# Split weights loaded from the GpSimd queue, and the whole output projection's weights split ahead of time

## The chip, the cores and the metric

The kernel runs on one core of one Trainium2 chip. The metric is the device time of one execution in microseconds (us). Three timed executions of the kernel before took 1645.35, 1647.06 and 1647.79 us.

## What is computed

One layer of a hybrid decoder trunk, for a batch of one, 2048 tokens and a model width of 1024, all in float32. In short, without the two mixers' insides:

```python
h = rmsnorm(x, norm_pre)
proj = h @ w_in                                   # 1024 -> 6416 columns
...
y_ssd = rmsnorm(ssd(...) * silu(z_ssd), ssd_norm) # Mamba-2 chunked scan, 16 heads x 64, in 2 groups
y_sc = sc_b * causal_dwconv(sc_c * sc_h, sc_conv_w) * silu(z_sc)
mix = jnp.concatenate([y_ssd, y_sc], axis=-1) @ w_out      # 2048 -> 1024
x = x + rmsnorm(mix, norm_post)
gate = jax.nn.sigmoid(x @ w_ple_gate)             # 1024 -> 1024
return x + gate * (p_i @ w_ple_proj)              # 256 -> 1024
```

`rmsnorm` divides by the root of the mean square over the width and multiplies by a weight.

## The kernel before

Activations stand transposed: 128 of the width on the partitions, 512 tokens (`TG`) along a row; there are four token groups. A float32 product is made of three products of rounded halves: each operand is split into a high part (a cast to fp32r on ACT, L146, L215, L543) and a low part (a subtraction on DVE, L147, L216, L546), and TensorE (PE) runs high x high, high x low and low x high (`PASSES`). A product with a 512-token group is thus twelve matmuls for four 128x128 blocks of weights. A *piece* is the split pair of such four blocks, 512 KB.

The stages, in the order of time:

- The **start** (`first_input`): warm-up products on a constant tile (`warm`, 14 of them, L452), then the projection of the per-layer embeddings `p` (`A_ple`), while the first tokens come in and their squares are summed (L425).
- The **input projection**, in two blocks of 1024 tokens, as 2x2 Strassen-Winograd products (seven for eight): for each block thirteen groups of one or two output tiles, each with seven products. Its weights come raw from HBM over SP's queue and are split on the way. While the groups 1 to 9 of the second block run (without the one for the scan's B and C), the generator `later_weights` is advanced by seven steps a group: it combines and splits the gate's weights and stores the pieces in HBM (`sg_d`), then splits the half of the output projection's weights that belongs to the short convolution and stores these (`so_d`, two pieces for each output tile).
- The **scan**, with the first half of the output projection in between (`under`, products `os`, weights `ws_os` read from `so_d`); its results go to HBM (`part_d`).
- The **output projection's second half** (`out_proj`, products `mo`): for a pair of token groups, eight output tiles each, two at a time. Its weights (`ws_o`) are loaded raw and split for each of the two pairs. Each result is evacuated with the stored part by DVE (`x`, L1217), then squared (ACT) and added to `ssq` (DVE, L1223).
- The **post-norm** (`norm`, L1233): for each token group the column sums of `ssq`, as four products with one column of ones, then root and reciprocal; the result goes through HBM and is spread over the partitions. `residual` (L1247, L1250) then adds the input `xres`.
- The **gate** (`gate_seven`), again seven products for eight, for two pairs of token groups: 28 pieces each (`GATES`), all read from `sg_d`. `finish` adds (L1288), takes the tanh (L1286, L1289), multiplies with the projected embeddings `pe` and adds `x` (L1291, L1292), and stores the result.

What sets the order: `Weights` holds all weights of the kernel as one sequence (`seq`) and six slots. `next` hands out a piece and starts the loads for the slots that are free by then; a load waits until PE has read the slot's last piece. All these loads are on SP's queue, which issues in order: with the loads of `part`, `xres`, `pe` and of the raw activations (L864), and the stores of the output (L1293). From the output projection on, `plan` lists at which unit (a step of `out_proj` or of the gate) the steps of norm, residual and gate operands are issued. A scheduler at build time puts each engine's instructions in an order by its own model of their durations; where the code says "in the order of the trace", an added edge keeps it from moving an instruction ahead.

## Time and profile before

| | us |
|---|---|
| median of three executions | 1647.06 (1645.35 to 1647.79) |
| the profiled execution | 1644.86 |
| its span on the core | 1643.2 |
| PE busy | 1628.1 |
| DVE busy | 1272.1 |
| ACT busy | 805.4 |
| POOL (GpSimd) busy | 49.6 |

All rows are of one profiled execution. Times are in us from the start of the span, unless marked ns. PE is the matmul engine and PEld its weight load, which runs beside it; DVE is VectorE, ACT ScalarE, POOL GpSimd, SP SyncE; SPq marks what an engine's queue issues or waits for. A row of a group has the line of the kernel, the engine, the operation, the names of what it writes and reads, the count, busy us and mean ns; a row of one tile has minimum, median and maximum ns, and the first and the last start. In a row of the timeline come start, length, engine, line, operation, and in brackets the idle time before it with what ended it. Matmuls overlap, and their ends are modelled: the time of a matmul is read from the distance of starts.

### The profile page before, as it was taken

The page shows a single profiled execution, that of the slowest core. Times are in us where ns is not written, and L with a number is a line of the kernel's source. Part 1 is how long each engine was busy: PE and PEld are TensorE (multiplying, and loading weights), DVE is VectorE, ACT ScalarE, POOL GpSimd, SP SyncE. Part 2 cuts the span into 40 slices and gives each one's busy share as a digit, 9 for nine tenths or more (in the row PEclk, how much of TensorE's full clock was granted, in tenths as well). Part 3 has the DMA queues.
Part 4 walks back from the last instruction along what each step waited for, and adds up shares of the span by engine and source line. Part 5 has one row for each costly group of instructions (what it writes and reads, how often), then busy time and mean ns, then how long its engine had stood idle before and what let it go on. Part 6 is the DMA issues. An engine that isn't in the chain of part 4 may idle for free.

```text
span 1643.2 us, 22720 instructions
## 1 busy us (share of the span) xinstructions
PE 1628.1 (99%) x8264; PEld 1339.9 (82%) x8264; DVE 1272.1 (77%) x1909; ACT 805.4 (49%) x1450; POOL 49.6 (3%) x71
## 2 busy tenths in 40 slices
PE   9999999999999999999999999999999999999998
PEld 8888888888888888888888888888788788887786
DVE  6997777987769978878978668477787736687785
ACT  8663444434337444554545335557757424234342
POOL 0000000000000100010010001000000000000000
PEclk9999999999999999999999999999999999999999
DMA  9452321774225334645765226878888535547996
GB/s 316 152 198 79 102 99 59 257 240 163 79 71 184 111 127 169 219 143 167 243 214 195 66 66 224 306 268 311 294 304 319 200 102 183 162 155 258 317 319 219
DMA packets 135620, 314.72 MB, mean 192 GB/s; under 512 B 18762, under 2 KB 20298, under 8 KB 135508
## 3 DMA queue, kind: packets, MB, share of 16 engines
q1 hardware_dynamic: 128596, 296.49, 53.5%
q10 hardware_dynamic: 6912, 16.78, 2.6%
q8 instruction: 65, 1.06, 0.3%
q14 instruction: 47, 0.39, 0.1%
HBM read 221.81 MB, written 91.41 MB: 191 GB/s over the span
## 4 chain that ended last, share of the span: by engine, by line
PE 90%; DVE 4%; DMA 3%; ACT 1%; issue 1%; SPq 0%; ACTq 0%; DVEq 0%
PE mo L226 9%; PE os L825 8%; PE mg_X L1315 5%; PE mg_Y L1315 4%; PE py L825 2%; PE A_ple L226 2%; PE A_xs1X L322 1%; PE A_xs2X L322 1%; PE A_gc6X L322 1%; PE A_gb7X L322 1%; PE A_gb5X L322 1%; PE A_gc7X L322 1%; PE A_z3X L322 1%; PE A_xs3X L322 1%; PE A_gb6X L322 1%; PE A_gc5X L322 1%
## 5 line engine op out<-in xcount | busy, mean ns | idle before, releaser
L825 PE MATMUL os<-act_m,ws_os 128*128 128x512 f32 x768 | 183.2, 394 | 0.7 <-ACT A_z L757 0.7
L226 PE MATMUL mo<-act_m,ws_o 128*128 128x512 f32 x768 | 178.0, 392 | 2.2 <-DVE x L1217 2.2
L226 PEld LDWEIGHTS mo<-act_m,ws_o 128*128 128x128 f32 x768 | 142.9, 188 | 36.2 <-DVE x L1217 5.1
L825 PEld LDWEIGHTS os<-act_m,ws_os 128*128 128x128 f32 x768 | 141.8, 188 | 34.3 <-issue 4.2
L1315 PE MATMUL mg_X<-act_x2s,ws_g 128*128 128x512 f32 x384 | 90.8, 393 | 0.7 <-ACT gth L1286 0.7
L146 ACT CAST ws_A_gc<-wr_A_gc 128x512 fp32r<-128x512 f32 x96 | 59.8, 623 | 56.9 <-PE A_gc5X L322 8.3
L1315 PEld LDWEIGHTS mg_X<-act_x2s,ws_g 128*128 128x128 f32 x384 | 70.9, 188 | 18.6 <-ACT gth L1286 1.7
L147 DVE TENSOR_TENSOR ws_A_gb<-wr_A_gb,ws_A_gb 128x512 fp32r<-128x512 f32 x96 | 66.0, 687 | 25.6 <-ACT ws_A_gb L146 25.4
L146 ACT CAST ws_A_gb<-wr_A_gb 128x512 fp32r<-128x512 f32 x96 | 59.6, 621 | 49.2 <-PE A_cb0Y L322 4.3
L676 DVE SCALAR_TENSOR_TENSOR xo<-ux,cols,xo 128x1024 f32<-128x1024 f32 x60 | 76.6, 1280 | 5.0 <-ACT xo L672 3.9
L1077 ACT ACTIVATE m<-m,adt 128x128 f32<-128x128 f32 x256 | 78.4, 390 | 0.9
L147 DVE TENSOR_TENSOR ws_A_gc<-wr_A_gc,ws_A_gc 128x512 fp32r<-128x512 f32 x96 | 66.0, 687 | 12.7 <-ACT ws_A_gc L146 11.8
L1315 PE MATMUL mg_Y<-act_x2s,ws_g 128*128 128x512 f32 x288 | 67.9, 392 | 1.4 <-DVE x L1250 1.4
L1315 PEld LDWEIGHTS mg_Y<-act_x2s,ws_g 128*128 128x128 f32 x288 | 53.5, 188 | 14.1 <-DVE x L1250 1.8
L1080 DVE SCALAR_TENSOR_TENSOR m<-m,gsb 128x1024 f32<-128x1024 f32 x32 | 38.2, 1222 | 25.4 <-ACT m L1077 25.4
L1217 DVE TENSOR_TENSOR x<-mo,part 128x512 f32<-128x512 f32 x32 | 22.1, 689 | 41.2 <-PE mo L226 41.0
L146 ACT CAST ws_A_xs<-wr_A_xs 128x512 fp32r<-128x512 f32 x48 | 29.9, 623 | 42.5 <-PE A_gc3X L322 8.4
L146 ACT CAST ws_A_z<-wr_A_z 128x512 fp32r<-128x512 f32 x48 | 29.9, 623 | 41.1 <-DVE wr_A_z L199 12.9
L1222 ACT ACTIVATE sq<-x 128x512 f32<-128x512 f32 x28 | 17.7, 633 | 63.4 <-DVE x L1217 63.3
L215 ACT CAST act_m<-mraw 128x512 fp32r<-128x512 f32 x64 | 37.4, 620 | 22.0 <-DVE mraw L880 10.1
L147 DVE TENSOR_TENSOR ws_A_z<-wr_A_z,ws_A_z 128x512 fp32r<-128x512 f32 x48 | 32.9, 686 | 18.4 <-ACT ws_A_z L146 18.4
L226 PE MATMUL A_ple<-act_p,ws_p 128*128 128x512 f32 x192 | 46.0, 397 | 0.0
(523 smaller groups left out, 3721.6 us busy)
## 6 DMA issues: line engine op xcount, KB each, us to landing
ws_g<-sg_d SPq DMA_DIRECT2D x56, 512.0 KB, 4.9
wr_A_gc<-in_w_t_dram SPq DMA_DIRECT2D x64, 256.0 KB, 2.7
wr_A_gb<-in_w_t_dram SPq DMA_DIRECT2D x64, 256.0 KB, 2.8
ws_os<-so_d SPq DMA_DIRECT2D x32, 512.0 KB, 5.8
m<-acs_d SPq DMA_DIRECT2D x32, 512.0 KB, 6.3
sg_d<-A_gs SPq DMA_DIRECT2D x28, 512.0 KB, 3.8
ple_d<-A_pe SPq DMA_DIRECT2D x32, 256.0 KB, 4.3
wr_A_xs<-in_w_t_dram SPq DMA_DIRECT2D x32, 256.0 KB, 3.6
```

Of the source, the lines that this page charges most:

```text
L146: S.copy(sp[:, 0, :kn, :], raw[:, :kn, :])
L147: V.tensor_tensor(sp[:, 1, :kn, :], raw[:, :kn, :], sp[:, 0, :kn, :].bitcast(F32), ALU.subtract)
L215: S.copy(a[:, 0, :], src)
L226: TE.matmul(out, sp[:, a, (k0 + k) % 4, :], act[k0 + k][:, b, :], start=k0 + k == 0 and q == 0, stop=k0 + k == n - 1 and q == 2)
L322: self.product = TE.matmul(out, sp[:, a, k % 4, :], t[:, b, ts_], start=p in OPENS and k == 0 and q == 0, stop=k == nk - 1 and q == 2, ski ...
L676: V.scalar_tensor_tensor(o, u[:, q:q + TB], col(w0 + q), o, ALU.mult, ALU.add)
L825: inst = f(*a, **k)
L1077: S.activation(m[:, c, :], m[:, c, :], AF.Exp, bias=nacs[b][:, h, c:c + 1])
L1080: V.scalar_tensor_tensor(mf, mf, 1.0, s["gsb"][gr], ALU.min, ALU.mult)
L1217: evac.append(V.tensor_tensor(x2[d], ps[:, i, :], pt[:, i, :], ALU.add))
L1222: S.activation(sq, x2[d], AF.Square)
L1315: TE.matmul(out, sp[:, a, k, :], ops_[t, p][k][:, b, :], start=p in OPENS and m_ == 0, stop=m_ == 11, skip_group_check=True)
```

## The change

It does five things.

- **Pieces of the output projection.** `so_d` has four pieces for each output tile. `later_weights` splits and stores all of them, first those of the short convolution, then those of the scan; it is advanced in groups 1 to 11 instead of 1 to 9. In the output projection's second half, pieces are loaded ready-made instead of raw, so the splits there go.
- **The queue of the pieces.** The loads of these pieces and of the gate's pieces are issued by GpSimd instead of SP.
- **The norm's sums.** `ssq` is split as well, into two tiles in which the columns that one product needs stand side by side; each product is two fp32r matmuls with two columns of ones.
- **The start.** The first four raw weights of the embeddings' projection are loaded from ACT's queue; nine warm-up products instead of 14.
- **The end.** The last output tile is finished in two halves.

```diff
-    so_d = [dram.tile([2, P, 2, TG], F32, name=f"so_d{d}") for d in range(KD)]
+    so_d = [dram.tile([4, P, 2, TG], F32, name=f"so_d{d}") for d in range(KD)]
...
+    ones_r = const.tile([P, 2], F32R, name="ones_r")
+    S.copy(ones_r, ones_d[:, 0:2])
...
-    def stored(src, name):
-
-        return name, lambda sp: nc.sync.dma_start(sp.bitcast(F32).rearrange("p a k c -> p a (k c)"), src)
+    def stored(src, name, by=nc.sync):
+
+        return name, lambda sp: by.dma_start(sp.bitcast(F32).rearrange("p a k c -> p a (k c)"), src)
...
-    seq = [direct(w_p[d], f"p_{d}", praw) for d in range(KD)]
+    seq = [direct(w_p[d], f"p_{d}", praw, S if d < 4 else nc.sync) for d in range(KD)]
...
     for t in range(0, NG, 2):
-        seq += [stored(so_d[d][q], f"os{t}_{d}_{q}") for d in range(KD) for q in range(2)]
+        seq += [stored(so_d[d][q], f"os{t}_{d}_{q}") for d in range(KD) for q in (2, 3)]
     for t in range(0, NG, 2):
-        seq += [direct(w_o[d, :, 4 * q:4 * q + 4, :], f"o{t}_{d}_{q}", praw) for d in range(KD) for q in (0, 1)]
+        seq += [stored(so_d[d][q], f"o{t}_{d}_{q}", G) for d in range(KD) for q in (0, 1)]
     for t in range(0, NG, 2):
-        seq += [stored(sg_d[n][p - 1], f"g{t}_{p}_{n}") for p, n in GATES]
+        seq += [stored(sg_d[n][p - 1], f"g{t}_{p}_{n}", G) for p, n in GATES]
...
-            for _ in range(14):
+            for _ in range(9):
                 TE.matmul(warm[:, 0:P], ones_d, ones_d, start=True, stop=True)
...
-            for n in range(2 * KD + 3):
-                if n < 2 * KD:
-                    d, q = divmod(n, 2)
+            parts = [(d, q) for h in (2, 0) for d in range(KD) for q in (h, h + 1)]
+            for n in range(len(parts) + 3):
+                if n < len(parts):
+                    d, q = parts[n]
...
                 if n >= 3:
-                    d, q = divmod(n - 3, 2)
+                    d, q = parts[n - 3]
                     keep(so_d[d][q], ahead[n - 3], f"A_os{d}_{q}")
...
-            elif b and 0 < n < 10 and ("cb", 0) not in prs:
+            elif b and 0 < n < 12 and ("cb", 0) not in prs:
                 mean = (next(gw, None) for _ in range(7))
...
                 ssq = ssq_[tg].rearrange("k (p c) -> k c p", c=TG // P)
+                hi, lo = (praw.tile([P, 4, P], F32R, tag="wraw", name=f"ssq2{n}_{tg}") for n in ("h", "l"))
+                S.copy(hi, ssq)
+                V.tensor_tensor(lo, ssq, hi.bitcast(F32), ALU.subtract)
                 ps = mm_bank(f"pn2_{tg}")
                 for c in range(TG // P):
-                    TE.matmul(ps[:, c:c + 1], ssq[:, c, :], ones_d[:, 0:1], start=True, stop=True)
+                    for n, part in enumerate((hi, lo)):
+                        TE.matmul(ps[:, 2 * c:2 * c + 2], part[:, c, :], ones_r, start=n == 0, stop=n == 1)
...
-            def finish(tg, d, in0, in1):
-                th = in1
+            def finish(tg, d, in0, in1, parts=1):
+                th, i = in1, d % 2
...
+                for n in range(parts):
+                    c = slice(n * TG // parts, (n + 1) * TG // parts)
+                    S.activation(th[:, c], in0[:, c], AF.Tanh, scale=0.5)
+                    evac.append(V.scalar_tensor_tensor(th[:, c], th[:, c], 1.0, L.get("pe", tg, d - i)[:, i, c], ALU.add,
+                                                       ALU.mult))
+                    V.scalar_tensor_tensor(th[:, c], th[:, c], 0.5, x2s_[tg][d][:, c], ALU.mult, ALU.add)
+                    nc.sync.dma_start(outT[d, :, tg * TG:(tg + 1) * TG][:, c], th[:, c])
...
-                    finish(*at(p, n), out, keep.get(({2: 1, 3: 6, 7: 5, 4: 0}[p], n)))
+                    finish(*at(p, n), out, keep.get(({2: 1, 3: 6, 7: 5, 4: 0}[p], n)), 1 + (t > 0 and m == len(GATES) - 1))
```

More of the change, by code (lines that the diff above doesn't have):

```diff
@@ L137, in next, with load_w @@
             return self.ready.pop(0)
-    def load_w(src, name, pool):
+    def load_w(src, name, pool, by=nc.sync):
         kn, cn = src.shape[1:]
         raw = pool.tile([P, 4, P], F32, tag="wraw", name=f"wr_{name}")
-        nc.sync.dma_start(raw[:, :kn, :cn], src)
+        by.dma_start(raw[:, :kn, :cn], src)
         return raw
@@ L147, in split_w, with direct @@
         V.tensor_tensor(sp[:, 1, :kn, :], raw[:, :kn, :], sp[:, 0, :kn, :].bitcast(F32), ALU.subtract)
-    def direct(src, name, pool):
-        return name, lambda sp: split_w(sp, load_w(src, name, pool), src.shape[1])
-    def stored(src, name):
-        return name, lambda sp: nc.sync.dma_start(sp.bitcast(F32).rearrange("p a k c -> p a (k c)"), src)
+    def direct(src, name, pool, by=nc.sync):
+        return name, lambda sp: split_w(sp, load_w(src, name, pool, by), src.shape[1])
+    def stored(src, name, by=nc.sync):
+        return name, lambda sp: by.dma_start(sp.bitcast(F32).rearrange("p a k c -> p a (k c)"), src)
     def split_dt(halves, name, pool):
@@ L565, in later_weights @@
             ahead = []
-            for n in range(2 * KD + 3):
-                if n < 2 * KD:
-                    d, q = divmod(n, 2)
+            parts = [(d, q) for h in (2, 0) for d in range(KD) for q in (h, h + 1)]
+            for n in range(len(parts) + 3):
+                if n < len(parts):
+                    d, q = parts[n]
                     ahead.append(A.ph.tile([P, TG], F32, tag="h2", name=f"A_o{d}_{q}"))
-                    nc.sync.dma_start(ahead[n].rearrange("p (k c) -> p k c", c=P),
-                                      w_o[d, :, 4 * (q + 2):4 * (q + 2) + 4, :])
+                    nc.sync.dma_start(ahead[n].rearrange("p (k c) -> p k c", c=P), w_o[d, :, 4 * q:4 * q + 4, :])
                 if n >= 3:
-                    d, q = divmod(n - 3, 2)
+                    d, q = parts[n - 3]
                     keep(so_d[d][q], ahead[n - 3], f"A_os{d}_{q}")
@@ L1280, in gate_seven @@
             bank, keep = {}, {}
-            def finish(tg, d, in0, in1):
-                th = in1
+            def finish(tg, d, in0, in1, parts=1):
+                th, i = in1, d % 2
                 if in1 is None:
                     th = tmp(f"gth_{tg}_{d}")
-                    S.activation(th, in0, AF.Tanh, scale=0.5)
                 else:
                     V.tensor_tensor(th, in0, in1, ALU.add)
-                    S.activation(th, th, AF.Tanh, scale=0.5)
-                i = d % 2
-                evac.append(V.scalar_tensor_tensor(th, th, 1.0, L.get("pe", tg, d - i)[:, i, :], ALU.add, ALU.mult))
-                V.scalar_tensor_tensor(th, th, 0.5, x2s_[tg][d], ALU.mult, ALU.add)
-                nc.sync.dma_start(outT[d, :, tg * TG:(tg + 1) * TG], th)
+                    in0 = th
+                for n in range(parts):
[5 more added lines that the diff above has]
+                    nc.sync.dma_start(outT[d, :, tg * TG:(tg + 1) * TG][:, c], th[:, c])
             def at(p, n):
```

2 lines of the change are left out of this document (1 added, 1 removed).

## The prediction

> **What bounds the kernel now.** I read the page's totals and its chain first, then the windows of the late stages, then the waits of PE from 1290 us on.
>
> ```profile
> PE 1628.1 (99%) x8264; PEld 1339.9 (82%) x8264; DVE 1272.1 (77%) x1909; ACT 805.4 (49%) x1450; POOL 49.6 (3%) x71
> ...
> PE 90%; DVE 4%; DMA 3%; ACT 1%; issue 1%; SPq 0%; ACTq 0%; DVEq 0%
> ...
> 801.60:839.60 38.00, 38.00 (x169) 31.47 (x168) 34.81 (x50) 23.21 (x39) 0.58 (x1) 1.00 0.83 268
> ...
> 877.70:915.80 38.10, 38.10 (x172) 31.43 (x171) 29.86 (x40) 18.11 (x29) 0.58 (x1) 1.00 0.38 130
> 915.80:953.90 38.10, 38.10 (x169) 31.54 (x169) 25.09 (x39) 14.06 (x26) 0.59 (x1) 1.00 0.23 71
> ...
> 1478.00:1560.00 82.00, 80.62 (x351) 65.40 (x351) 60.50 (x98) 30.83 (x53) 0.00 (x0) 1.00 0.85 284
> 1560.00:1638.00 78.00, 76.99 (x334) 61.34 (x332) 56.65 (x90) 28.02 (x48) 0.00 (x0) 1.00 0.83 284
> ...
> PE mo L226 <- DVE x L1217: 2.2, 3, 1.4
> PE mg_Y L1315 <- DVE x L1250: 1.4, 1, 1.4
> PE mg_X L1315 <- ACT gth L1286: 0.7, 1, 0.7
> ```
>
> TensorE is busy 99% and carries 90% of the chain. So an edit counts only if it takes work off PE or removes one of the few moments in which PE stands. Work that DVE or ACT lose is worth nothing by itself. In the window rows the columns are PE, PEld, DVE, ACT and POOL busy, then granted clock (1.00), DMA share and GB/s. The last three rows name all waits of PE in the last 350 us: 4.3 us in five places. That is the most that the stage with the most edits can give through waits.
>
> **The change, part by part.**
>
> *The output projection's weights (`later_weights`, `seq`).* Removed from the output projection: 32 casts on ACT and 32 subtractions on DVE. Added in the second block of the input projection: half as many, each with one load and one store.
>
> ```profile
> L147 DVE TENSOR_TENSOR ws_o<-wr_o,ws_o 128x512 fp32r<-128x512 f32 x32 | 21.7, 688 | 10.0 <-ACT ws_o L146 9.9
> ...
> L543 ACT CAST A_os<-A_o x16: 602/616/622, 787.0 to 869.9; 128x512 fp32r<-128x512 f32 x16
> L546 DVE TENSOR_TENSOR A_os<-A_o,A_os x16: 679/684/689, 791.5 to 873.1; 128x512 fp32r<-128x512 f32 x16
> ...
> 1297.13 1.66 ACT L146 CAST ws_o<-wr_o 128x512 fp32r<-128x512 f32 x3
> 1299.74 2.50 DVE L147 TENSOR_TENSOR ws_o<-wr_o,ws_o 128x512 fp32r<-128x512 f32 x4
> 1302.15 0.69 DVE L1217 TENSOR_TENSOR x<-mo,part 128x512 f32<-128x512 f32 x1
> 1302.90 10.27 PE L226 MATMUL mo<-act_m,ws_o 128*128 128x512 f32 x44 [1.44 <-DVE x L1217]
> ```
>
> The sixteen splits that are there now end at 873, and the new ones follow in the next two groups, 877.7 to 953.9. In those two windows DVE is idle 8.2 and 13.0 us, ACT 20 and 24, DMA share is 0.38 and 0.23. Seven or so splits a group add 7 x 0.684 = 4.8 us of DVE and 7 x 0.616 = 4.3 of ACT: under cover, 0. If the cover were gone it would be at most the 16 x 0.684 = 11 us of DVE. SP's queue takes 16 more stores that each wait for a split, and the input weights are queued behind those; the same pattern runs from 787 to 873 now, and from 801.6 to 839.6 PE is full (38.00 of 38).
>
> In the output projection the gain is one stall. At 1302.9 PE waits 1.44 us for the first evacuation `x`, and that evacuation sits behind four weight splits of 2.50 us on DVE. With the splits gone it is free to run from 1299.7 on, before PE stands at 1302.90 - 1.44 = 1301.46: 1.4 us less. The two shorter waits on L1217 (2.2 - 1.4 = 0.8 in total) I leave in. Bounds: 0 to 2.2.
>
> *The sums of squares of the post-norm (`norm`, L1233).* This is work on PE itself.
>
> ```profile
> L226 PEld LDWEIGHTS mo<-act_m,ws_o 128*128 128x128 f32 x768 | 142.9, 188 | 36.2 <-DVE x L1217 5.1
> ...
> L1233 PEld LDWEIGHTS pn<-ones_d,ssq x32: 308/329/332, 1390.2 to 1493.5; 128*128 128x128 f32 x32
> ...
> L425 PEld LDWEIGHTS A_ssq<-ones_d,ssq x16: 186/192/192, 23.3 to 36.8; 128*128 128x128 f32 x16
> ...
> 1390.41 1.80 PE L1233 MATMUL pn<-ones_d,ssq 128*128 128x1 f32 x8
> 1392.08 2.15 PE L226 MATMUL mo<-act_m,ws_o 128*128 128x512 f32 x8
> ...
> 23.30 1.05 PE L425 MATMUL A_ssq<-ones_d,ssq 128*128 128x1 f32 x8
> 24.22 1.17 PE L226 MATMUL A_ple<-act_p,ws_p 128*128 128x512 f32 x4
> ...
> 1377.10 0.68 DVE L1223 TENSOR_TENSOR ssq<-ssq,sq 128x512 f32<-128x512 f32 x1
> ```
>
> Each of the four norms issues four fp32 products with one column, which the trace shows as eight matmuls. From the first of them to the next ordinary matmul it is 1392.08 - 1390.41 = 1.67 us. L425 is the same product in the same number of passes, and takes 24.22 - 23.30 = 0.92 us. The difference in the code is the weight operand: L1233 reads every fourth column of `ssq` and its weight load takes 329 ns, L425 reads neighbouring columns and takes 192 ns. The change copies `ssq` into two gathered tiles, so its weights lie side by side, and it issues eight fp32r products with two columns: also eight passes. I take L425's cost: 4 x (1.67 - 0.92) = 3.0 us less on PE. The trace has no fp32r product this narrow. If its passes cost as L1233's do, the gain is 0; if half of L425's, it is 4 x (1.67 - 0.46) = 4.8. I stay at 3.0: the fp32r weights of the big products load in 188 ns, nearest to L425.
>
> The change puts one ACT copy and one DVE subtraction ahead of these products: 0.62 + 0.69 us by the rows of L543 and L147 above. In the quoted case the last addition into `ssq` of token group 0 ends at 1377.8 and its products start at 1390.4, so there are 12 us for 1.3 us. What is queued behind them on DVE is ordinary evacuation. Cost 0; the rival below says what it is otherwise.
>
> *Gate pieces and second-half pieces loaded by GpSimd.* The gate's 56 loads keep their bytes; the output projection's 32 load a split pair, twice the bytes of the raw weights that they replace.
>
> ```profile
> 131.59 2.72 PE A_xs0X L322 x12
> ...
> L154 SPq DMA_DIRECT2D ws_g<-sg_d x56: 319/320/1187, 1453.6 to 1621.1; - x56
> ...
> DMA to landing us min/median/max: 4.4/5.6/8.0
> ...
> 1508.63 0.38 SPq L864 DMA_DIRECT2D xres<-in_xT_dram  x1
> 1509.11 7.25 SPq L154 DMA_DIRECT2D ws_g<-sg_d  x4
> ...
> 1510.53 0.33 SPq L154 DMA_DIRECT2D ws_g<-sg_d  x1
> ...
> 1517.38 2.97 PE L1315 MATMUL mg_Y<-act_x2s,ws_g 128*128 128x512 f32 x12 [1.38 <-DVE x L1250]
> ```
>
> Twelve matmuls on one gate piece last 2.72 us. Six slots give a load a lead of up to 5 x 2.72 = 13.6 us if it is issued as soon as its slot is free, and landing takes 8.0 at the worst. On SP it is not issued then: before 1517.38 the queue stood until 1508.63 to issue `xres`, whose buffer had to be given back, and the `ws_g` load issued at 1510.53 lands, at 5.6 to 8.0 us, between 1516.1 and 1518.5. That covers 1517.3, when PE goes on. The wait's row names L1250, but the queue order says that the late piece is at least as likely; both go if SP is free of gate loads, for then `xres` and the pieces no longer stand behind one another. I take the 1.4 us as gone (bounds 0 to 1.4).
>
> POOL issues no DMA in this trace. By SP's rows the issue of one such load costs 0.32 to 1.19 us of the issuer, and even 1.19 is less than 2.72, so POOL, which is idle in these windows, keeps up: 0. On POOL's queue only the next pieces stand behind a piece that waits for its slot.
>
> The Trainium skill (DMA: Bandwidth & Descriptors, section Issuing engines are not separate DMA queues) says that starting DMAs on several engines only saves the sequencer's time to start them. By that rule alone the 1.4 us would be 0 and the result 1642.8; the row speaks against it here, since what the pieces lose on SP is not issue time but the wait of a neighbour in the queue.
>
> *Start.*
>
> ```profile
> 5.67 1.15 ACT L146 CAST ws_p<-wr_p 128x256 fp32r<-128x256 f32 x3 [0.63 <-DMA wr_p<-in_w_p_dram]
> ...
> 6.12 3.23 PE L226 MATMUL A_ple<-act_p,ws_p 128*128 128x512 f32 x11
> ...
> 55.00:95.00 40.00, 39.26 (x174) 32.20 (x173) 39.14 (x65) 25.27 (x45) 0.39 (x1) 1.00 0.45 155
> ```
>
> The first four embedding weights move to ACT's queue, and five warm-up products go. ACT now waits 0.63 us for these weights; PE can start about that much earlier than 6.12. But from 55 to 95 DVE is busy 39.14 of 40 us, and it will not be earlier by as much. I take 0.3 of it (bounds -0.5, if ACT's four issues delay its first casts, to 1.0).
>
> *Tail.*
>
> ```profile
> 1637.71 0.60 ACT L1286 ACTIVATE gth<-mg_X 128x512 f32<-128x512 f32 x1 [3.10 <-PE mg_X L1315]
> ...
> 1639.07 0.69 DVE L1292 SCALAR_TENSOR_TENSOR gth<-gth,x 128x512 f32<-128x512 f32 x1
> ...
> L146 ACT CAST ws_p<-wr_p x8: 394/406/409, 5.7 to 43.2; 128x256 fp32r<-128x256 f32 x8
> L147 DVE TENSOR_TENSOR ws_p<-wr_p,ws_p x8: 418/422/426, 6.1 to 43.7; 128x256 fp32r<-128x256 f32 x8
> ```
>
> The last tile is finished in two halves. Now it takes 1639.76 - 1637.71 = 2.05 us to the last store's issue. Halves cost about 0.41 on ACT and 0.42 on DVE; one ACT half and four DVE halves in a row are 2.1 us, overlapped a little less, and the last store carries half the bytes. I take 0.1 (bounds -0.3 to 0.5).
>
> **Sum**, against the profiled execution, whose time is 1644.86 (span 1643.2 and 1.66 around it): 3.0 + 1.4 + 1.4 + 0.3 + 0.1 = 6.2 us. All instructions of ACT and DVE get a new order, and a kernel without slack on PE will show some new short wait; for that I give back 0.5, the size of one of the two short waits on L1217. So 5.7 us less: 1639.2 for such an execution. The median of the three runs, 1647.06, is 2.2 above it, and timings are compared by medians: 1647.06 - 5.7 = 1641.4.
>
> **Rivals.**
>
> *Waits only move.* The evacuation of the output projection and of the gates stays as it is, DMA share stays 0.83 to 0.85, and the two 1.4 us waits come back at another place. Then only PE's own work counts: 1647.06 - 3.0 = 1644.1. For it speaks that the two waits have a DVE instruction as their last link, and DVE is busy 73% there (56.65 of 78). Chance 0.14.
>
> *The split stands in front of PE.* The products of the norm wait for the copy and subtraction, because these are queued behind the evacuation of the current unit: 4 x 1.3 = 5.2 us lost, sum -0.5, 1646.6. Against it stand the 12 us. Chance 0.07.
>
> *GpSimd does not keep up: slower.* If preparing a load on POOL advances only while DVE is idle, which is 27% of the time in the gates, a load of p us takes p / 0.27, and PE starves from p = 0.27 x 2.72 = 0.73 us on. SP's rows have the price at 0.32 typical and 1.19 at most, on both sides of this. Halfway between 0.73 and 1.19, at 0.96, a piece would take 3.55 us, and 56 pieces lose 56 x 0.83 = 46 us: 1687. For it: nothing in the trace; POOL has never done this here. Against it: POOL's other work shares its time with a busy DVE now without PE standing. Chance 0.11. The Trainium skill (SBUF — State Buffer, sections SBUF: two separate sides, and Who interferes with whom) describes such a block: GpSimd writes the descriptors itself and cannot while VectorE holds the port that they share; but it limits this to VectorE's two-port modes, and says tensor_tensor has none. No run here shows it yet.
>
> **How the numbers follow.** The forecast has 0.68, within 1638 to 1643.7. A difference of 0.2%, 3.3 us, is about what a measurement of this kernel can tell from none: the limit is 1643.8. Faster: 0.64 of the forecast's 0.68 and 0.06 of the first rival, 0.70. Same: the rest of both and the second rival, 0.17. Slower: the third rival with 0.11 and 0.02 for a cover that fails, 0.13. The range takes in the two rivals on the near side, up to 1646.5, and below it the upper ends of norm, start and the short waits: 1637.
>
> **What would show it.** Right: eight `pn` matmuls in about 0.9 us, four times; no wait of 1.4 us near 1303 and 1517; POOL issuing 88 loads with pieces ahead; DVE busy some 5 us more in two of the 38 us windows, PE still full there. Wrong: PE waiting for `ws_g` or `ws_o` landings all through the gates; a wait of PE before `pn`; PE holes between 880 and 955.

## The result and the profile after

| | us |
|---|---|
| kernel before, median of 6 executions | 1647.42 (1645.31 to 1649.23) |
| changed kernel, median of 6 executions | 1658.31 (1654.70 to 1662.05) |
| ratio, 95% interval | 1.0074 (1.0062 to 1.0087) |
| profiled execution after; its span | 1660.16; 1658.5 |

The change makes the kernel slower, by 0.74% (12.2 us) in the ratio and by 11 us between the medians. The forecast was 5.7 us faster, with 1637.0 to 1646.5 as the range; the result lies 12 us above its upper end. One execution of run 12 below took 3792.81 us and is left out of its row.

The page after, busy time by engine and the granted clock in 40 slices:

```profile
PE 1631.8 (98%) x8254; PEld 1340.6 (81%) x8254; DVE 1265.0 (76%) x1899; ACT 796.8 (48%) x1440; POOL 112.4 (7%) x159
...
PEclk9999999999999999999999999999999899999999
...
PE 79%; DVE 6%; issue 6%; DMA 5%; ACT 2%; POOL 1%; SPq 0%; DVEq 0%; POOLq 0%; ACTq 0%
```

DVE and ACT have less to do, as predicted, and PE does no more matmuls than before, yet its busy time grew by 3.7 us: some matmuls ran slower, and one slice shows a clock of 8 tenths. In the chain, PE fell from 90% to 79%; DVE, DMA and plain issue took its place.

From 1285 us on, the waits of PE after are these; before they were 4.3 us in five places:

```profile
PE mo L228 <- DVE x L1218: 8.9, 5, 4.4
PE mg_Y L1322 <- DVE act_x2s L218: 2.4, 1, 2.4
PE mo L228 <- ACT act_m L217: 2.1, 1, 2.1
PE mg_Y L1322 <- DMA ws_g<-sg_d: 1.0, 1, 1.0
PE mg_X L1322 <- ACT gth L1296: 0.7, 1, 0.7
PE mo L228 <- DVE act_m L218: 0.7, 1, 0.7
```

That is 15.8 us. Where the two traces part can be read from the starts of matching matmuls. The output projection starts at 1293.81 before and at 1292.80 after, 1.0 us earlier; the last product of the kernel ends at 1637.7 and 1653.5. The stretch from the first product of the output projection to the last product of all, 343.9 us before, is 16.8 us longer in this trace. So the whole loss lies behind 1293 us. In the two windows of the added splits, 877.7 to 953.9, DVE is 2.0 and 4.4 us busier than before, and PE has one hole of 0.62 us, at 916.2; by 1293 it is made good. This stretch is used below as a measure of one trace.

The first hole, in the timeline after (SP's queue, GpSimd's issues, DVE and PE):

```profile
1286.60 0.53 POOL L156 DMA_DIRECT2D ws_o<-so_d  x1 [2.19 <-PE os L826]
1287.23 0.36 SPq L865 DMA_DIRECT2D mraw<-yz_d  x1
1289.32 0.53 POOL L156 DMA_DIRECT2D ws_o<-so_d  x1 [2.19 <-PE os L826]
1293.26 0.53 POOL L156 DMA_DIRECT2D ws_o<-so_d  x1 [3.41 <-PE os L826]
...
1297.65 1.42 DVE L881 SCALAR_TENSOR_TENSOR mraw<-mraw,cols,gn 128x512 f32<-128x512 f32 x2 [4.45 <-DMA mraw<-yz_d]
...
1299.11 0.62 PE L228 MATMUL mo<-act_m,ws_o 128*128 128x512 f32 x1 [2.07 <-ACT act_m L217]
1299.65 6.11 DVE L218 TENSOR_TENSOR act_m<-mraw,act_m 128x512 fp32r<-128x512 f32 x10
...
1305.84 0.69 DVE L1218 TENSOR_TENSOR x<-mo,part 128x512 f32<-128x512 f32 x1
```

The last raw activations (mraw) are issued by SP at 1287.23. While they are under way GpSimd issues a weight piece of 512 KB at 1289.32 and another at 1293.26; PE needs those two only from 1323.5 on. The activations are there by 1297.65, 10.4 us after their issue. DVE stands 4.45 us for them, then has ten subtractions to do, and the first evacuation `x` comes at 1305.84 instead of 1302.15.

### The profile page after: what moved, and what is told of

Read it like the earlier page. It is cut to its first block, busy times and chain, and to the rows that moved or that the text cites. A ratio compares the mean times of both kernels' runs of the same rounds, so it can differ in the third digit from the quotient of the medians.

```text
span 1658.5 us, 22766 instructions
## 1 busy us (share of the span) xinstructions
PE 1631.8 (98%) x8254; PEld 1340.6 (81%) x8254; DVE 1265.0 (76%) x1899; ACT 796.8 (48%) x1440; POOL 112.4 (7%) x159
## 3 DMA queue, kind: packets, MB, share of 16 engines
q8 instruction: 65, 1.06, 0.3%
## 4 chain that ended last, share of the span: by engine, by line
PE 79%; DVE 6%; issue 6%; DMA 5%; ACT 2%; POOL 1%; SPq 0%; DVEq 0%; POOLq 0%; ACTq 0%
PE mo L228 8%; PE os L826 7%; PE A_ple L228 2%; PE py L826 2%; PE mg_X L1322 2%; DMA mraw<-yz_d 2%; PE mg_Y L1322 2%; PE A_xs1X L324 1%; PE A_gb7X L324 1%; PE A_gc7X L324 1%; PE A_z3X L324 1%; PE A_xs3X L324 1%; PE A_gb6X L324 1%; PE A_gb4X L324 1%; PE A_gc4X L324 1%
## 5 line engine op out<-in xcount | busy, mean ns | idle before, releaser
L228 PE MATMUL mo<-act_m,ws_o 128*128 128x512 f32 x768 | 184.8, 402 | 11.6 <-DVE x L1218 8.9
L228 PEld LDWEIGHTS mo<-act_m,ws_o 128*128 128x128 f32 x768 | 147.1, 193 | 48.4 <-DVE x L1218 14.0
L1322 PEld LDWEIGHTS mg_X<-act_x2s,ws_g 128*128 128x128 f32 x384 | 70.8, 188 | 18.6 <-ACT gth L1296 1.7
L1322 PEld LDWEIGHTS mg_Y<-act_x2s,ws_g 128*128 128x128 f32 x288 | 54.6, 192 | 16.8 <-DVE act_x2s L218 4.2
```

The lines of the kernel that those rows point to most:

```text
L228: TE.matmul(out, sp[:, a, (k0 + k) % 4, :], act[k0 + k][:, b, :], start=k0 + k == 0 and q == 0, stop=k0 + k == n - 1 and q == 2)
L1322: TE.matmul(out, sp[:, a, k, :], ops_[t, p][k][:, b, :], start=p in OPENS and m_ == 0, stop=m_ == 11, skip_group_check=True)
```

## The theories and the experiments

Theory Q: GpSimd's queue starts pieces as soon as a slot is free, and so lets them run beside loads of SP that are needed sooner (mraw, part, xres). These land late, and everything that stands behind them in DVE's queue is late too. Theory N: the split of the sums of squares stands in front of evacuations. Theory O: the stored pieces cost by themselves, by twice the bytes or by the order that the build gives to ACT and DVE once the splits are gone.

Ratios are to the kernel before, run on the same chip (its medians beside 1 to 18 were 1644.8 to 1646.4). "Stretch" is that from the first product of the output projection to the last product, against the 343.9 us of before. "mraw" is the time of one load, the last raw activations issued before the output projection (the one at 1287.23 above), from its issue to the instruction of DVE that waits for it; before it was 5.7 us. Both are from one trace each.

| kernel | median us | ratio (95%) | stretch | mraw us |
|---|---|---|---|---|
| changed kernel | 1658.31 | 1.0074 (1.0062 to 1.0087) | +16.8 | 10.4 |
| 1 changed, all pieces by SP | 1649.69 | 1.0021 (1.0009 to 1.0032) | +4.6 | 5.5 |
| 2 changed, old norm | 1656.75 | 1.0076 (1.0046 to 1.0106) | +12.9 | 8.9 |
| 3 changed, old weights of the output projection | 1651.31 | 1.0038 (1.0017 to 1.0058) | +5.7 | 5.4 |
| 4 before, split norm | 1645.38 | 0.9999 (0.9988 to 1.0009) | +0.7 | 6.2 |
| 5 changed, gates by SP | 1653.30 | 1.0057 (1.0038 to 1.0076) | +9.3 | 7.9 |
| 6 changed, output projection by SP | 1652.84 | 1.0048 (1.0031 to 1.0065) | +8.2 | 6.5 |
| 7 before, new start | 1651.58 | 1.0037 (1.0024 to 1.0050) | +2.3 | 5.4 |
| 8 before, gathered sums, tail in halves | 1646.61 | 1.0005 (0.9995 to 1.0014) | +1.0 | 6.1 |
| 9 before, extra traffic by GpSimd | 1665.49 | 1.0123 (1.0106 to 1.0140) | +18.6 | 9.9 |
| 10 changed, pieces held behind mraw | 1656.03 | 1.0062 (1.0047 to 1.0077) | +14.4 | 8.1 |
| 11 as 8, pe behind part | 1644.67 | 0.9998 (0.9988 to 1.0007) | +0.2 | 6.1 |
| 12 stored pieces by SP, old start, gathered sums | 1652.08 | 1.0034 (1.0023 to 1.0045) | +3.9 | 6.1 |
| 13 before, stored pieces by SP | 1654.04 | 1.0046 (1.0030 to 1.0063) | +9.6 | 5.6 |
| 14 before, stored pieces by GpSimd | 1656.57 | 1.0056 (1.0042 to 1.0070) | +14.6 | 9.2 |
| 15 before, gates by GpSimd | 1647.80 | 1.0011 (0.9997 to 1.0025) | +1.0 | 5.7 |
| 16 changed, old start | 1657.11 | 1.0063 (1.0038 to 1.0087) | +10.9 | 8.9 |
| 17 before, weight bytes twice | 1650.36 | 1.0029 (1.0020 to 1.0039) | -1.1 | 5.3 |
| 18 as 13, DVE's order by hand | 1652.73 | 1.0044 (1.0027 to 1.0060) | +7.2 | 5.4 |

In the six kernels whose output projection's pieces come from GpSimd (the changed one, 2, 5, 10, 14, 16) the load of mraw takes 7.9 to 10.4 us, in the others 5.3 to 6.5, except for 9. The medians of mraw in the expectations below are of another kind: with pieces on GpSimd and in the kernel before, the trace gives the landing of one load alone, near 1385 us, so 8.1 and 5.3 are single loads, while 5.7 is of six in run 1. That one load took 6.1 us in 1.

### The queue

**1, all pieces by SP.**

```diff
-        seq += [stored(so_d[d][q], f"o{t}_{d}_{q}", G) for d in range(KD) for q in (0, 1)]
+        seq += [stored(so_d[d][q], f"o{t}_{d}_{q}") for d in range(KD) for q in (0, 1)]
...
-        seq += [stored(sg_d[n][p - 1], f"g{t}_{p}_{n}", G) for p, n in GATES]
+        seq += [stored(sg_d[n][p - 1], f"g{t}_{p}_{n}") for p, n in GATES]
```

> The changed kernel with one thing undone: the pieces of the output projection and of the gates are started by SP again instead of GpSimd; the split sums of squares, the stored pieces, start and tail stay as changed. Theory Q (GpSimd's own queue lets the pieces run beside urgent loads of SP, mraw, part and xres, and makes those land late): most of the loss comes back, 1648 to 1651 us, and the gaps of PE at 1299 to 1307, 1429 and 1530 go. Theory N (the split of the sums of squares stands in front of evacuations): nothing comes back, 1657 to 1660, and the 4.4 us gap near 1402 stays. Theory O (the stored pieces, twice the bytes, and the new order of ACT and DVE that their absence of splits brings): nothing comes back or it gets worse, since SP then also carries 88 more pieces, 1656 to 1663.

Of 12.2 us 8.7 come back (0.53%), in Q's band. Not all the holes that Q named go: the one for act_m near 1299 is gone and that near 1429 is 0.63 us, but PE stands 3.15 us at 1303, 2.89 at 1397.9 and 1.67 at 1521.7. PE, DVE and ACT do the same instructions in nearly the same order, so the same load can be compared. In the timeline of this kernel:

```profile
1287.16 0.36 SPq L865 DMA_DIRECT2D mraw<-yz_d  x1
1287.62 2.56 SPq L156 DMA_DIRECT2D ws_o<-so_d  x3
...
1292.63 1.41 DVE L881 SCALAR_TENSOR_TENSOR mraw<-mraw,cols,gn 128x512 f32<-128x512 f32 x2 [0.50 <-DMA mraw<-yz_d]
...
1298.15 0.33 ACTq L946 DMA_DIRECT2D part_d<-po  x1
...
1302.51 0.69 DVE L1218 TENSOR_TENSOR x<-mo,part 128x512 f32<-128x512 f32 x1 [1.79 <-issue]
1303.25 89.42 PE L228 MATMUL mo<-act_m,ws_o 128*128 128x512 f32 x380 [3.15 <-DVE x L1218]
```

The same mraw load is issued at 1287.16 and is there by 1292.63: 5.5 us instead of 10.4. The pieces are the same and as many; they stand behind it in SP's queue. The hole of 3.15 us at 1303 has another cause: DVE is idle for 1.79 us, and the evacuation starts just after the last `po` store of the stage before has landed (1298.15 and 4.2 us for this store is 1302.35). The same holds in 6 (1298.74 and 4.3 us, `x` at 1303.19), 12 (1302.47 and 5.1, 1307.78), 13 (1298.26 and 5.2, 1303.64) and 18 (1296.16 and 5.2, 1301.54). The profile names no releaser here ("issue"); that it is this store is read from the five matches and from the code, where the pool of `x` is opened when that of `po` is closed, and no run tests it.

**9, traffic alone.** In mix_pair, behind the split of a raw activation:

```diff
+            if k < KD:
+                G.dma_start(spare_d[k + i], acts_o[tg][k + i].bitcast(F32))
```

> The kernel before, with the order of PE, DVE, ACT and SP left as it is, plus 24 transfers of 512 KB started by GpSimd: each split activation of the output projection is also stored to a scratch buffer in DRAM that nobody reads, as soon as it is ready. Theory Q, in the sharp form that it is the traffic beside SP's loads that makes mraw and part late: mraw's median landing rises from 5.3 us to 7 or more, PE gets new gaps near 1300 and near 1370 to 1420, 1649 to 1655. If the new order of the instructions is what costs, or something about pieces that GpSimd loads: as before, 1644 to 1646, and no new gap.

20 us more, beyond what was expected. The order of every other engine is that of the kernel before, line by line, and no wait of PE, DVE or ACT is put down to the new stores, so nothing but traffic is new. The load of mraw ahead of the output projection takes 9.9 us instead of 5.7. The waits of DVE for mraw between 1285 and 1430 and those of PE behind 1285:

```profile
DVE mraw L881 <- DMA mraw<-yz_d: 25.0, 7, 7.2
...
PE mo L227 <- DVE x L1220: 9.2, 3, 5.1
PE mo L227 <- ACT act_m L216: 3.5, 2, 2.9
PE mo L227 <- DVE act_m L217: 1.2, 3, 0.8
```

DVE's wait was 7.7 us in six places before. These are the holes of the changed kernel (`x`, act_m), only larger. This run shows that traffic which GpSimd starts beside urgent loads makes them late. The same traffic from the queue of another engine, ACT's for one, was not run.

**5 and 6, one half of the pieces each.** Only the gates' line, or only the output projection's line, of the diff of 1.

> The changed kernel with the gates' 56 pieces started by SP again; the output projection's 32 pieces stay on GpSimd. Theory Q, by the waits seen so far: the 2.6 and 1.2 us gaps of the gates near 1530 and 1610 shrink to one of about 1.7 near 1520, but mraw still lands 8 us or later (median from issue to landing 8.1 us in the changed kernel, 5.7 with everything on SP), and the gaps of the output projection near 1299 to 1307, 1402 and 1429 stay: 1654 to 1657. If the gates' pieces carry the loss: 1648 to 1651.

> The changed kernel with the output projection's 32 pieces started by SP again; the gates' 56 stay on GpSimd. Theory Q: mraw lands in about 5.7 us as with everything on SP, the gaps of the output projection are those of that kernel (3.2 near 1303, 2.9 near 1398), and the gates wait for ws_g twice, 2 to 4 us in total: 1649.5 to 1652. If the gates' pieces carry the loss: 1655 to 1658.

Either half back on SP gives some of it: 2.8 us (0.17%) for the gates, 4.3 (0.26%) for the output projection, and both 8.7. 5 came in 0.7 us under its band, 6 0.8 above. The interval of 5 overlaps that of the changed kernel widely, that of 6 by a little, so the gates' share is not told from nothing by these times. In 6 PE waits for ws_g twice, 1.62 us at 1523.8 and 1.16 at 1602.6.

**10, pieces held behind the activations.** Behind each load of mraw (the late ones, in another place of the code, likewise):

```diff
+            if kind == "mraw" and at[1] < KD:
+                G.tensor_copy(seen, t[:, 0, 0:1])
```

> The changed kernel, where GpSimd first copies one column of each raw activation tile (mraw) as it lands, ahead of the pieces that follow in its queue, so that those pieces start only when the activations are there; everything else stays on GpSimd. Theory Q: mraw lands in 5 to 6.5 us again, the gap of 2.1 us for act_m near 1299 goes, and the time comes to that of the kernel with the output projection's pieces on SP, 1650 to 1654. If the pieces' being on GpSimd costs by itself: 1656 to 1660.

A miss by 2 us. The load of mraw at the boundary came down from 10.4 to 8.1 us only, not to the 5 to 6.5 expected, and that near 1388 to 6.2. The wait for act_m of 2.07 us became one of 0.61; but PE then stood 4.03 us for the first `x`, until 1304, and 2.21 and 0.97 us for ws_g in the gates. Holding pieces back in this way is not enough to get the time.

**15, the gates' pieces on GpSimd alone.** The gates' line of the change in the kernel before.

> The kernel before with the gates' 56 pieces started by GpSimd and nothing else; the other engines keep their order but for a few lines. The prediction had 1.4 us less here. Theory Q, by the two waits for ws_g of 1 to 2.5 us that all kernels with these pieces on GpSimd show: 1 to 3 us more, 1646.5 to 1648.5, with two waits of PE for ws_g near 1517 and 1597.

The time is undecided (-0.03% to +0.25%). In the trace the first product of the gates starts 1.3 us earlier than before and the last product of all ends 0.1 us later, so the gates cost 1.4 us more. The waits of PE there:

```profile
1516.22 19.65 PE L1315 MATMUL mg_Y<-act_x2s,ws_g 128*128 128x512 f32 x84 [1.47 <-DMA ws_g<-sg_d]
1595.01 19.67 PE L1315 MATMUL mg_Y<-act_x2s,ws_g 128*128 128x512 f32 x84 [1.02 <-DMA ws_g<-sg_d]
```

Before there was one wait, 1.38 us at 1517, beside the 0.69 us at the end that both kernels have. It came back at the same place under another name, and a second one joined it.

### The stored pieces

**3, the old weights in the changed kernel.** `later_weights`, `so_d` and the line of `seq` as before.

> The changed kernel with one thing undone: the first half of the output projection's weights is loaded raw by SP and split on ACT and DVE as before, and no more pieces are stored ahead in the input projection; the gates' pieces stay on GpSimd, the split sums of squares, start and tail stay as changed. Theory O: the loss in the output projection goes, 1648 to 1651, with the old 1.4 us wait near 1303. Theory Q: the gaps at 1299 to 1307 and 1429 go (there are no pieces on GpSimd's queue there), that at 1530 stays: 1651 to 1654. Theory N: the gap near 1402 stays, 1655 to 1659.

6 us of 12 come back, with 2.37 and 1.44 us of waits for ws_g left in the gates. That is in Q's band, at its lower end, and 0.3 us above O's, so the two are not told apart by it.

**13 and 14, the stored pieces alone, by SP and by GpSimd.**

```diff
-        seq += [direct(w_o[d, :, 4 * q:4 * q + 4, :], f"o{t}_{d}_{q}", praw) for d in range(KD) for q in (0, 1)]
+        seq += [stored(so_d[d][q], f"o{t}_{d}_{q}") for d in range(KD) for q in (0, 1)]
...
-            elif b and 0 < n < 10 and ("cb", 0) not in prs:
+            elif b and 0 < n < 12 and ("cb", 0) not in prs:
```

> The kernel before with one part of the change alone: all weights of the output projection split once in the input projection and stored, and the second use's pieces (512 KB instead of 256) started by SP. If the stored pieces cost by their bytes and by the order that they bring: 3 to 5 us more than before, 1648 to 1650, as the changed kernel with everything on SP was. If it is the start and the split norm that kept that kernel above before: 1644 to 1646.

> As the run before this one, but the 32 stored pieces are started by GpSimd; DVE and ACT keep the same order but for a line or two. Theory Q: mraw lands later than in the run before (median 8 us against 5 to 6), and it is 3 to 6 us slower than it: 1652 to 1655. If the queue makes no difference: as the run before, within 1.

With SP alone, without GpSimd, this part of the change costs 0.46%, 7.6 us. GpSimd adds 0.10%, 1.6 us, which the intervals do not tell from nothing; the two traces differ by 5.0 us of stretch, and mraw takes 9.2 against 5.6 us. So theory O has a share of its own, and in this kernel the larger one. The first hole with SP alone, in its timeline (ACT, DVE and PE):

```profile
1298.26 0.33 ACTq L945 DMA_DIRECT2D part_d<-po  x1
...
1303.64 0.69 DVE L1217 TENSOR_TENSOR x<-mo,part 128x512 f32<-128x512 f32 x1 [2.82 <-issue]
...
1304.38 89.94 PE L226 MATMUL mo<-act_m,ws_o 128*128 128x512 f32 x380 [4.71 <-DVE x L1217]
...
1390.77 1.41 DVE L880 SCALAR_TENSOR_TENSOR mraw<-mraw,cols,gn 128x512 f32<-128x512 f32 x2 [4.30 <-DMA mraw<-yz_d]
```

DVE has no split to do here, and stands 2.82 us all the same. The splits that the prediction took for the cause of the wait at 1303 were only the last link that the trace showed: behind them lay the end of the stage before (po and its store), and that is what PE waits for now, 4.71 us instead of 1.44. The last row leads to the next hole, 1.17 us at 1398: mraw in front of `x` in DVE's queue.

**17, the bytes twice, and 18, DVE's order by hand.**

```diff
+            raw = load_w(src, name, pool)
+            nc.sync.dma_start(spare_d[n % 8], src)
+            split_w(sp, raw)
```

> The kernel before with the order of PE, DVE and ACT left as it is, and each raw weight piece of the output projection moved a second time by SP (256 KB from DRAM to a scratch buffer in DRAM, right behind its load), so that the stage moves as many bytes for weights as with stored pieces. If the stored pieces cost by their bytes: mraw's landing rises from 5.3 us, first evacuations and parts come late, 3 to 8 us more than before, 1649 to 1654. If they cost by the order that the build gives to ACT and DVE once the splits are gone: 1645 to 1647.

17 missed its place: nothing ties the extra copies to the output projection, so SP issued all 32 between 57 and 107 us. There they cost 7.5 us in the trace with PE, DVE and ACT in the order of before; in the output projection nothing was added, and nothing lost (-1.1). The window from 54 to 90 us of this kernel, columns as in the prediction:

```profile
54.00:90.00 36.00, 33.78 (x141) 27.15 (x140) 32.26 (x54) 19.68 (x36) 0.00 (x0) 0.95 0.86 258
```

Before, the DMA share there was 0.38, the clock 1.00, and PE did 156 matmuls. So extra copies cost PE time there too; but they stand in SP's queue in front of loads of the weights, so traffic and queue are not told apart, and whether the bytes make the stored pieces dear is not answered.

```diff
+                if evac:
+                    tc.add_manual_dep(scaled_.ins, evac[-1].ins.name, NOSYNC, reason="behind the evacuation")
```

> The kernel with the stored pieces by SP alone (7.6 us above before), with one order set by hand on DVE: the scaling of the raw activations for the next token groups comes behind the last evacuation that was written before it, so that no evacuation x stands behind the landing of mraw in DVE's queue, as it did from 1386 to 1397 there (DVE idle 4.3 us for mraw, then x late, PE standing 1.2 us and then slow). If that order is the cost after 1380: 3 to 4 us less than without it, 1648 to 1651, the gap near 1304 staying. If it is the landing itself, that the next products wait for: the gap comes back as a wait for act_m, 1652 to 1656.

DVE's wait for mraw went from 9.5 to 0.8 us, but the time is that of 13 within the intervals, and the hole at 1302 stays with 3.36 us. The order behind mraw is not what most of the 7.6 us hang on.

### The norm, the start, and a version to beat both

**2 and 4, the norm undone and the norm alone.**

```diff
-                    for n, part in enumerate((hi, lo)):
-                        TE.matmul(ps[:, 2 * c:2 * c + 2], part[:, c, :], ones_r, start=n == 0, stop=n == 1)
+                    TE.matmul(ps[:, c:c + 1], ssq[:, c, :], ones_d[:, 0:1], start=True, stop=True)
```

> The changed kernel with one thing undone: the sums of squares of the post-norm are summed as before, by four fp32 products with every fourth column as weights, without the copy and the subtraction. Theory N: the 4.4 us gap near 1402 with its half-speed matmuls after it goes, 7 us back less the 3.4 us that the slow products cost, 1653 to 1656, and every other gap stays. Theories Q and O: the products cost their 4 x 0.86 us again and nothing else moves, 1660 to 1662.

> The kernel before with one part of the change alone: the sums of squares are split on ACT and DVE and summed by eight fp32r products. By the prediction: 3 us less than before, 1644.4. Theory N: 4 x 0.86 us won on PE and a gap of 4 us or more at one of the norms at least, 1647 to 1651. Theories Q and O: as the prediction, 1644 to 1645.

Neither undoing it nor doing it alone moves the time, and 2 lies between its two bands. The products did get cheaper; after, the first of them and the matmul behind them:

```profile
1395.73 0.17 PE L1238 MATMUL pn<-ones_r,ssq2h 128*128 128x2 f32 x1
...
1396.54 1.65 PE L228 MATMUL mo<-act_m,ws_o 128*128 128x512 f32 x6
```

0.81 us instead of 1.67, so 3.4 us in four norms. But the split stands in front of an evacuation, as theory N says. After, DVE, ACT and PE at the second norm:

```profile
1399.21 0.62 ACT L217 CAST act_m<-mraw 128x512 fp32r<-128x512 f32 x1 [0.62 <-DVE mraw L881]
1399.76 1.11 ACT L1233 CAST ssq2h<-ssq 128x512 fp32r<-128x512 f32 x1
...
1400.90 1.06 DVE L1234 TENSOR_TENSOR ssq2l<-ssq,ssq2h 128x512 fp32r<-128x512 f32 x1 [0.35 <-ACT ssq2h L1233]
1401.88 0.68 DVE L1218 TENSOR_TENSOR x<-mo,part 128x512 f32<-128x512 f32 x1
...
1402.61 9.63 PE L228 MATMUL mo<-act_m,ws_o 128*128 128x512 f32 x29 [4.42 <-DVE x L1218]
```

`x` waits for 0.35 + 1.06 us of the split, and that in turn for late activations. In 2 this hole is 1.47 us instead of 4.42: 3 us back, and the 3.4 us of the old products to pay. In 4 the gain goes to a hole of 2.17 us at 1303 with slow matmuls behind it and one of 1.70 at 1418.

**8 and 11, sums without ACT and DVE.** GpSimd gathers the sums, four fp32 products as before; the tail in halves. 11 also orders the gate's first pe loads behind an urgent one.

```diff
+                ssq = praw.tile([P, 4, P], F32, tag="wraw", name=f"ssq2c_{tg}")
+                G.tensor_copy(ssq, ssq_[tg].rearrange("k (p c) -> k c p", c=TG // P))
...
+            if kind == "pe" and urgent_:
+                tc.add_manual_dep(load.ins, urgent_[-1].ins.name, NOSYNC, reason="behind the urgent loads")
+            elif kind == "part" and at == (2, 2):
+                urgent_.append(load)
```

> The kernel before with two things: the sums of squares are copied by GpSimd into a gathered fp32 tile (one copy, nothing on ACT or DVE) ahead of the same four fp32 products, and the last gate tile is finished in two halves. If the weights that lie side by side are what makes the products fast, each norm costs 0.9 us of PE instead of 1.67, 3.0 us in total, and the tail gives 0.5 us: 1642. Against it: GpSimd's copy could take several us and make PE wait before the products, or the new order brings a new stall as in the run with the split norm alone, where 3.4 us were won on PE and lost again: 1645. Theory N has nothing to say against this kernel, since nothing of the norm is queued in front of an evacuation.

> The kernel before with the norm's gathered copy on GpSimd, the tail in two halves, and one order set by hand: the gate's first loads of pe come behind the load of the third unit's part in SP's queue. In the run without that order, part was issued at 1411.0 right behind two such loads and the stage's rs, landed after 5.4 us instead of 3.8, and PE stood 1.8 us at 1417. If traffic beside an urgent load is what makes it late, that gap goes to 0.5 or less: 1.3 to 1.8 us less than without it, 0.1 to 0.3% below the kernel before, 1642 to 1644. If the gap is set by something else (the release of part's buffer): no change, 1645 to 1647.

The layout is what made the old products slow: the same fp32 products on gathered weights take 1403.40 - 1402.59 = 0.81 us. Yet the time does not move. In 8, DVE, SP and PE at 1410 to 1417:

```profile
1410.58 0.33 SPq L1240 DMA_DIRECT2D rs<-rs_d  x1
1411.01 0.38 SPq L864 DMA_DIRECT2D part<-part_d  x1
...
1416.46 0.69 DVE L1217 TENSOR_TENSOR x<-mo,part 128x512 f32<-128x512 f32 x1 [1.96 <-DMA part<-part_d]
...
1417.30 2.97 PE L226 MATMUL mo<-act_m,ws_o 128*128 128x512 f32 x12 [1.81 <-DVE x L1217]
```

PE comes sooner, and then waits for part, which took 5.4 us to land. With pe behind part, 11, that hole is gone, as expected; the trace has others instead (2.17 us at 1305.8, 1.08 at 1385.6), and the median of 1644.67 is not to be told from before. No version here beats the kernel before by more than the interval.

**7 and 16, the start alone and the start undone.**

```diff
-    seq = [direct(w_p[d], f"p_{d}", praw) for d in range(KD)]
+    seq = [direct(w_p[d], f"p_{d}", praw, S if d < 4 else nc.sync) for d in range(KD)]
...
-            for _ in range(14):
+            for _ in range(9):
```

> The kernel before with the start of the change alone: the first four embedding weights by ACT's queue, nine products to warm up instead of fourteen. The prediction had 0.3 us less. The stage marks of the kernels with this start say otherwise: their first product of the input projection at 54 us comes 0.5 to 1.5 us later than before, and the first product of the embedding 0.3 to 0.6 us later. So 0.3 to 1.5 us more than before, 1645.7 to 1647, read from the marks of the profile, since the times alone can hardly tell it; by the prediction 1645.1 and marks 0.3 us earlier.

> The changed kernel with the start undone: all embedding weights by SP, fourteen products to warm up. By the marks of the changed kernel its start costs 0.5 us there: 1657 to 1659. If the start costs the 5 to 6 us that it cost alone: 1651 to 1653.

Alone it costs 0.37%, 6.1 us: more than expected. ACT and PE in the first 10 us of 7:

```profile
0.81 1.86 ACTq L142 DMA_DIRECT2D wr_p<-in_w_p_dram  x4
2.70 1.28 ACT L146 ACT_TABLE_LOAD   x1 [2.70 <-issue]
...
8.72 0.40 ACT L146 CAST ws_p<-wr_p 128x256 fp32r<-128x256 f32 x1 [0.76 <-DMA wr_p<-in_w_p_dram]
9.03 2.18 ACT L215 CAST act_p<-A_p 128x512 fp32r<-128x512 f32 x4
...
9.69 18.85 PE L226 MATMUL A_ple<-act_p,ws_p 128*128 128x512 f32 x72 [4.81 <-ACT act_p L215]
```

ACT's queue got the four casts of the weights in front of the first cast of an activation, each behind the landing of its own load, and PE starts at 9.69 instead of 6.12; at 54 us it is 5.0 behind. In the changed kernel ACT's order is another, the start is 0.6 us late and 0.5 at 54 us, and undoing it gives 0.11%, 1.8 us, with intervals that overlap: little of the loss.

**12, all stored by SP, with the old start and the gathered sums.** The diffs of 1, 8 and 11 in the changed kernel, 7 undone.

> The changed kernel's stored pieces, all started by SP, with the start of before, the norm's gathered copy on GpSimd, the order of pe set by hand and the tail in two halves. With everything on SP the changed kernel was 3 to 4 us above the kernel before; the start is worth 1 to 2 of these by the stage marks, the split norm in front of an evacuation 1.4 to 2.9 (the gap near 1398). If these are all: 1644 to 1646, level with before. If the stored pieces themselves cost in the output projection (twice the bytes): 1647 to 1650.

Higher than either expectation. More than half of it is another hole: between the first products at 131 and at 1030 us it loses 5.1 us, all of it from 880 to 960 us, where the added splits lie (PE stands 3.74 us at 918.2); the changed kernel loses 0.3 there. The cover that the prediction named held in one of these two kernels and failed in the other. From the first product of the output projection on it loses 3.9, near the 4.6 of 1: so neither the start nor the split norm was what kept that kernel above before.

## Why the prediction was wrong

**The step that failed** is the one on pieces loaded by GpSimd: "POOL, which is idle in these windows, keeps up: 0. On POOL's queue only the next pieces stand behind a piece that waits for its slot." The first sentence held: an issue took 0.53 us of GpSimd, 88 times, and PE waited 1.0 us for a piece in all, so the third rival (1687) is out. But the step looked at who stands behind whom in a queue, and not at what shares the transfer engines. With all loads in SP's queue, as in 1, a piece for later is started after the load needed now. With a queue of its own it overtakes, and 512 KB that are there in 5.5 us with SP's order took 10.4. "Twice the bytes" was even named there, and priced at nothing. By 1 the queue is worth 8.7 us in the changed kernel; by 9 traffic alone can cost 20.

A second term failed beside it: the ready-made pieces were to give 1.4 us, and by 13 they cost 7.6 us on their own, before GpSimd has any part in it. Which of their effects costs this is open (below).

The sentence of the Trainium skill that the prediction set aside (DMA: Bandwidth & Descriptors, section Issuing engines are not separate DMA queues) was the better guide: transfers interleave on the same engines whoever starts them, and starting them elsewhere only saves issue time. The trace agrees, with 10.4 us for mraw in the changed kernel against 5.5 in 1, and goes further: the saving has a price, since the order of the one queue was what gave the urgent load its turn.

Point by point:

- Weights split ahead: nearly under cover in the input projection, as predicted (one hole of 0.62 us, and the output projection started 1.0 us earlier). The 1.4 us at 1303 were not won: behind the four splits lay the landing of the last po store and mraw. Sign wrong: holes of 2.07, 0.66 and 1.99 us between 1299 and 1307. The trace of before had the evidence, had one asked what DVE would have waited for next:

```profile
1296.74 0.33 ACTq L945 DMA_DIRECT2D part_d<-po  x1
```

The stores of po took 4.8 us there in the median. By that (an estimate) this one lands at about 1301.5, so `x` could have come some 0.6 us earlier, not 1.4.
- Norm: size right (0.81 us instead of the 0.92 forecast, 3.4 us in all), the cover wrong. The copy and the subtraction took 1.11 and 1.06 us, not 0.62 and 0.69, since they read every fourth element; and at one of the four norms they stood right in front of a late evacuation. The second rival had this mechanism.
- Gates: -1.4 forecast, about +1.4 in the trace of 15. The wait at 1517 was not the piece behind xres in SP's queue, or not it alone: before, DVE stands 1.04 us for xres itself. After, PE stands 2.43 us at 1530 for operands that wait for xres, issued from 1520.6 on and there at 1528.3, with three pieces issued by GpSimd in between. DVE before and after:

```profile
1514.71 0.69 DVE L1250 TENSOR_TENSOR x<-x,xres 128x512 f32<-128x512 f32 x1 [1.04 <-DMA xres<-in_xT_dram]
...
1528.31 0.69 DVE L1255 TENSOR_TENSOR x<-x,xres 128x512 f32<-128x512 f32 x1 [2.67 <-DMA xres<-in_xT_dram]
```

- Start: -0.3 forecast; +0.5 in the changed kernel's trace, +6 alone. Who issues a load was changed, but with it the order of ACT's queue.
- Tail: -0.1 forecast; -0.5 in the traces. From the start of the first ACT step behind the last product to the end of the span it was 1643.2 - 1637.71 = 5.5, and is 1658.5 - 1653.51 = 5.0:

```profile
1653.51 0.66 ACT L1296 ACTIVATE gth<-mg_X 128x256 f32<-128x256 f32 x2 [3.11 <-PE mg_X L1322]
```

- The first rival (waits only move) had the right idea with the wrong size: they moved and grew from 4.3 to 15.8 us.

**What stays open.** Why the stored pieces cost 7.6 us when SP loads them (13): by their bytes or by the build's order; 17 missed its place, and 18 rules out only one part of the order. And the parts do not add up: stored pieces by SP cost 0.46% alone, but only 0.21% with the norm, start and tail of the change around them; and GpSimd's queue costs 0.53% in the changed kernel, but only 0.10% for the stored pieces and 0.11% for the gates' when each is put into the kernel before, neither told from nothing. With orders set anew at every build, effects of one or two us have no fixed owner.

## What to carry to other kernels

A second DMA queue is not free bandwidth: before moving loads that run ahead off a queue, list the loads that are needed soonest at that time, because here the old queue's order was their priority; count the bytes in flight beside them, not only the issue time. When a wait is removed, ask of every input of the waiting instruction when it would have been ready, since the profile names only the last one. And when PE is 99% busy, a gain on PE is only worth what the loads behind it can follow: here 3 us won on PE gave nothing in 4 and 8.

## What the runs showed of the hardware

The granted clock falls to half behind some holes of PE, and a hole so costs more than its length. Rows of the windows behind holes, columns as before, of the changed kernel:

```profile
1300.30:1306.60 6.30, 4.22 (x10) 2.82 (x10) 6.14 (x11) 3.36 (x7) 0.00 (x0) 0.50 0.13 44
...
1402.60:1408.00 5.40, 5.39 (x13) 4.23 (x14) 5.33 (x9) 3.10 (x5) 0.00 (x0) 0.50 0.43 123
```

The first window lies behind holes of 2.07 and 0.66 us with one matmul between them, and 1.99 us of it are a hole again. Behind the hole of 4.42 us PE did 13 matmuls in 5.4 us, one in 0.427 us instead of 0.227: 2.6 us more. The clock was 0.66 behind the hole of 2.17 us in 4, and 0.64 behind that of 3.15 in 1:

```profile
1303.00:1308.00 5.00, 4.95 (x15) 3.91 (x16) 0.16 (x1) 0.63 (x1) 0.00 (x0) 0.66 0.57 184
```

But it stayed 1.00 behind 1.44 us in the kernel before, and behind 2.89 us in 1, at 1397.8:

```profile
1397.80:1403.00 5.20, 5.14 (x23) 4.25 (x24) 5.14 (x10) 3.12 (x5) 0.00 (x0) 1.00 0.43 134
```

The Trainium skill (TensorE: Matmul & The Clock Gate, section What's actually happening) has the clock halved after an idle window of about 3.4 us whose phase runs free. The clock of 0.50, and that not every hole is hit, agree with that; that 2.17 us were enough once does not fit an idle window of that length.

A copy or subtraction of 128x512 that reads every fourth element took 1.11 us on ACT, 1.06 on DVE and 1.54 on GpSimd in the mean of four (1.09 to 2.16); with neighbouring elements ACT and DVE take 0.62 and 0.69. A matmul's weight load took 329 ns from every fourth column and 192 from neighbouring ones, and the products followed.
